# A decoder layer in f32r: SBUF tiles that begin at shifted addresses

## The chip, the core and the metric

The kernel runs on one core of a Trainium2 chip. A core has a matrix engine (TensorE, PE in the profile, with its weight loads shown as PEld), VectorE (DVE), ScalarE (ACT), GpSimd (POOL) and SyncE (SP), which here issues nearly all DMAs. Operands lie in SBUF, 128 partitions wide; an address below is a place in bytes within a partition, the same in all 128. TensorE writes to PSUM.

The metric is the time of the whole kernel on the device in microseconds, median of several runs.

## The reference

One layer over x of 256 positions and 1024 channels, with a LayerNorm behind each of three parts:

```python
x = layer_norm(ALPHA * x + 0.5 * swiglu(x, ffn1_w_up, ffn1_w_down), ln1_g, ln1_b)
z = x @ w_in                       # q, k, v, h, g_b, g_c, gates: 8192 columns
y_attn = moba_attention(q, k, v) @ w_proj_attn      # 8 heads of 128, causal, one block of 256
y_conv = (g_b * short_conv(g_c * h, conv_w, conv_b)) @ w_proj_conv   # 3 taps per channel
g_attn, g_conv = split(sigmoid(gates + b_gate))
x = layer_norm(ALPHA * x + (g_attn * y_attn + g_conv * y_conv) @ w_out, ln2_g, ln2_b)
x = layer_norm(ALPHA * x + 0.5 * swiglu(x, ffn2_w_up, ffn2_w_down), ln3_g, ln3_b)
# swiglu(x, w_up, w_down) = (silu(gate) * up) @ w_down, hidden width 2816
```

All inputs are float32, and the weights are read once: 119.56 MB from HBM.

## The kernel before

**Numbers in two parts.** Each float32 factor is split into a high part, rounded to the type float32r (f32r below), and a low part, the rest. A product is three f32r matmuls: high by high, high by low, low by high. ScalarE makes the high part by a cast, VectorE the low part by a subtraction. For weights that is `prep` (L884 and L887), from a raw tile that a DMA has filled into two S tiles, hi and lo. For activations it is `split` (L203, L204) and `split_later` (L213, L208), into X tiles or T tiles.

**Tiles.** A `Slots` object (L49) hands out tiles of one kind from a pool with a fixed number of places, in turn. S: 10 tiles of 2048 words (8192 bytes) for weights, and q and k of the attention. X: 3 tiles of 4096 words (16,384 bytes) for transposed activations and v. RAW: 3 tiles of 2048 words for weights as they come from HBM. N: 9 tiles of 1032 words (4128 bytes) for rows of x, LayerNorm vectors, gates and the convolution. T: 8 tiles of 512 words (2048 bytes) for small things, among them the hidden activations of a feed-forward part. In SBUF the ten S tiles stand one behind the other, then the X, raw and T tiles, then identity, mask and small constants, then the N tiles.

**Matmuls.** `cols` (L346) holds weight columns still and streams activations: per unit of weights 16 matmuls of 512 columns (hi weights against both parts of X) and 16 of 256 columns (lo weights against the high part); in the profile these are `acc<-X,S`, the moving operand first. `rows` (L294) holds activations still and streams 512 weight columns (`acc<-S,X`). The down projection `D` (L437) holds a T tile still and streams S (`acc<-S,T`). All these matmuls stand in line 117. Transposes (L190) are float32 matmuls against the identity (`acc<-ident,N` and `acc<-ident,T`). All f32r operands are slices that begin at a multiple of 512 bytes within their tile.

**The convolution.** In `GC` (L566) an N tile holds u, four channel tiles of 258 words each (1032 bytes, a multiple of 32 and 8 more), two zeros ahead of 256 positions. L574 writes u behind the two zeros, so 8 bytes into it. L578 (ScalarE) reads it from there for the last tap, and L582 (VectorE) reads it from its start and from one word on for the other two.

**Order.** The program is put in an order by hand: the matmuls stand in a list with a modelled time each, `advance` and `prep` (L879 to L919) issue casts and subtractions some time ahead of the matmuls that need them, `defer` puts steps a little later. A raw tile is loaded as soon as one of the three places is free (L869). Nothing in this depends on addresses.

Of the kernel before, what the change touches and what calls it, by code (L numbers as in the profile page):

```python
# [29 lines left out]
S_BUFS, X_BUFS, RAW_BUFS, N_BUFS, T_BUFS, ACC_BUFS = 10, 3, 3, 9, 8, 8  # L30


class Op:


    def __init__(self, fn, cols, unit=None):
        self.fn, self.cols, self.unit, self.after = fn, cols, unit, []
# [11 lines left out]
class Slots:  # L49


    def __init__(self, pool, tag, shape, bufs):
        self.pool, self.tag, self.shape, self.bufs, self.live, self.n = pool, tag, shape, bufs, 0, 0

    def get(self, dt=F):
        assert self.live < self.bufs, self.tag
        self.live += 1
        self.n += 1
        return self.pool.tile(self.shape, dt, tag=self.tag, name=f"{self.tag}{self.n}", bufs=self.bufs)

    def free(self, n=1):
        self.live -= n
# [3 lines left out]
def layer(ctx: ExitStack, tc: tile.TileContext, a: dict, out: bass.AP):  # L66
    nc = tc.nc
    sb = ctx.enter_context(tc.tile_pool(name="sb", bufs=1))
    ps = ctx.enter_context(tc.tile_pool(name="ps", bufs=1, space=PSUM))
    ctx.enter_context(tc.manual_schedule())  # L70

    S = Slots(sb, "S", [128, 2048], S_BUFS)
    X = Slots(sb, "X", [128, 4096], X_BUFS)
    RAW = Slots(sb, "raw", [128, 2048], RAW_BUFS)
    N = Slots(sb, "N", [128, 1032], N_BUFS)
    T = Slots(sb, "T", [128, 512], T_BUFS)
    ACC = Slots(ps, "acc", [128, 512], ACC_BUFS)

    base, ins, units, sig, st = [], [], [], [], {}
# [3 lines left out]

    for pool in (S, X, RAW, T):
        pool.get()
        pool.free()


    still = T.get(R)
    nc.gpsimd.memset(still.bitcast(F), 0.0)  # L90
# [21 lines left out]
    def small(shape, name, bufs=2):  # L112
        return sb.tile(shape, F, name=name, bufs=bufs)


    def mm(dst, lhsT, rhs, start, stop, cols, unit=None):
        return Op(lambda: nc.tensor.matmul(dst(), lhsT=lhsT(), rhs=rhs(), start=start, stop=stop), cols, unit)  # L117

    def passes(dst, sta, mov, first, last, cols, unit=None):

        return [mm(dst, lambda x=x: sta(x), lambda w=w: mov(w), first and i == 0, last and i == 2, cols, unit)
                for i, (x, w) in enumerate(((0, 0), (0, 1), (1, 0)))]
# [95 lines left out]
    def xnew():  # L218
        return X.get(R).rearrange("p (k s t n) -> p k s t n", k=KT, s=2, t=2)

# [154 lines left out]
    def both(dst, bank):  # L375
        nc.scalar.copy(dst, bank[:, 256:512])  # L376
        nc.vector.tensor_tensor(dst, dst, bank[:, 0:256], op=OP.add)  # L377


    def ffn(key, wu, wd, ln_i, by_rows, order, tail, after_ln):  # L380
# [4 lines left out]
        def hT_of(j, kk):  # L385
            if ("hT", key, j, kk) not in st:
                st["hT", key, j, kk] = T.get(R).rearrange("p (s n) -> p s n", s=2)
            return st["hT", key, j, kk]

        def U_epi(j, t, bank):  # L390
            sc = T.get()
            nc.scalar.activation(sc[:, 0:256], bank[:, 0:256], AF.Silu)
            nc.vector.tensor_tensor(sc[:, 256:512], sc[:, 0:256], bank[:, 256:512], op=OP.mult)
            st["h", j, t] = sc

        def hT_put(j, t, at, dt):
            def evac(bank):
                T.free()
                for kk in range(2):
                    hT = hT_of(j, kk)[:, :, t * 128:(t + 1) * 128]  # L400
                    split(hT[:, 0], hT[:, 1], bank[:, kk * 128:(kk + 1) * 128])
# [14 lines left out]
        def U_cols(j):  # L416
            ug, uu = col_unit(wu, j * 256), col_unit(wu, DFF + j * 256)

            def gate(bank, b):
                g = T.get()  # L420
                both(g[:, 0:256], bank)
                defer(0.8, lambda: nc.scalar.activation(g[:, 0:256], g[:, 0:256], AF.Silu))  # L422
                st["g", j, b] = g
# [10 lines left out]
            if j == NJ - 1:  # L434
                base[-1].after.append(X.free)

# [91 lines left out]
    def V(c, t):  # L528
# [3 lines left out]
        def epi(bank):  # L532
            if c == 0 and t == 0:
                st["v"] = X.get(R).rearrange("p (s t n) -> p s t n", s=2, t=2)
            cs = slice(c * 512, (c + 1) * 512)
# [11 lines left out]
    def QK(kind, c):  # L547
        def epi(bank, j):
            if j == 0:
                state["hold"] -= 1  # L550
                st[kind, c] = S.get(R).rearrange("p (s h n) -> p s h n", s=2, h=4)
            t_ = T.get()
# [65 lines left out]
    def attention(head, at, dt):  # L618
# [5 lines left out]
        def bank(name, lo, hi):  # L624
            def f():
                if name not in box:
                    box[name] = ACC.get()
                return box[name][:, lo:hi]
            return f


        both_k = lambda: st["k", c][:, :, h, 0:128]
        ops = [mm(bank("S", 0, 256), lambda: qT(0, 0, 128), both_k, True, False, 256),
               mm(bank("S", 0, 128), lambda: qT(1, 0, 128), lambda: kT(0, 0, 128), False, True, 128)]
        ops += passes(bank("S", 256, 512), lambda s: qT(s, 128, 256), lambda w: kT(w, 0, 256), True, True, 256)

        def softmax():
            if head == 0:
                st["xT", "a"] = xnew()
            P = T.get()  # L640
            b = box["S"]
            mx = small([128, 2], "mx")
# [5 lines left out]
            ACC.free()  # L648
            nc.vector.reduce_max(mx[:, 0:1], P[:, 0:128], axis=mybir.AxisListType.X)
            nc.vector.reduce_max(mx[:, 1:2], P[:, 128:384], axis=mybir.AxisListType.X)  # L650
            nc.vector.tensor_scalar(mx, mx, -1.0, None, op0=OP.mult)
# [205 lines left out]
    order, need, clock, t = [], {}, [], 0.0  # L857
# [99 lines left out]
```

## Time and profile before

| | |
|---|---|
| median of 2 runs | 644.17 us (644.11 and 644.24) |
| the profiled execution, its own time | 644.08 us |
| its span, first to last instruction | 642.3 us |
| TensorE busy (matmuls) | 632.6 us, 98% of the span |
| VectorE, ScalarE, GpSimd busy | 71%, 56%, 3% |
| mean granted TensorE clock | 0.996 of 2.4 GHz |

The page of a profile shows one execution: busy time by engine, the span in 40 slices, the chain of work that ended last, and groups of instructions by line. Matmuls are pipelined: one begins before the last has ended, so the shown length of one (283 or 389 ns) is longer than the distance from start to start, the pitch. A row of the timeline merges neighbours of a kind: its start, its length up to the end of the last of them, and how many they are (xN). PE is busy nearly always here, so what counts is the pitch. Rows of a stretch (A:B in us from the span's start) give each engine's busy time in it and, in brackets, the instructions that touch it.

### The profile page before, as it was taken

What the parts mean: (1) busy time and instruction counts of PE and PEld (TensorE: products, weight loads), DVE (VectorE), ACT (ScalarE), POOL (GpSimd) and SP (SyncE); (2) the same over time, 40 slices, a digit from 0 to 9 for tenths busy, and PEclk for the clock granted to TensorE, in tenths of its full rate; (3) what the DMA queues carried; (4) which work ended last, traced back from release to release, by engine and by line L of the source; (5) the groups of instructions that cost most, each with busy time, mean ns of one, the idle gap of its engine ahead of it and who ended that gap; (6) DMA issues with size and microseconds to landing.
All of it is one profiled execution on the core that took longest, in us unless ns stands there. A gap on an engine that the chain in (4) does not pass through costs nothing.

```text
span 642.3 us, 8774 instructions
## 1 busy us (share of the span) xinstructions
PE 632.6 (98%) x3416; PEld 547.3 (85%) x3416; DVE 454.3 (71%) x731; ACT 356.8 (56%) x624; POOL 18.7 (3%) x27
## 2 busy tenths in 40 slices
PE   8999999999999999999999999999999999999995
PEld 6888888888888888888888888888888888888884
DVE  4786666666678577778879987886966666666636
ACT  5765555555534558676698664552556555555510
POOL 2000000000011000000000000001100000000002
PEclk9999999999999999999999999999999999999998
DMA  9766665567635572555666655572556755555301
GB/s 294 259 233 199 218 234 193 204 218 254 193 124 180 157 234 85 158 171 163 204 214 193 222 201 181 197 257 77 190 196 207 253 196 197 197 196 197 132 1 66
DMA packets 95854, 121.18 MB, mean 189 GB/s; under 512 B 2196, under 2 KB 84420, under 8 KB 95812
## 3 DMA queue, kind: packets, MB, share of 16 engines
q1 hardware_dynamic: 95668, 120.36, 57.4%
q8 instruction: 27, 0.44, 0.3%
q10 hardware_dynamic: 144, 0.26, 0.1%
q14 instruction: 15, 0.12, 0.1%
HBM read 119.56 MB, written 1.05 MB: 188 GB/s over the span
## 4 chain that ended last, share of the span: by engine, by line
PE 98%; POOL 0%; DVE 0%; issue 0%; ACT 0%; POOLq 0%; DVEq 0%
PE acc L117 96%; PE acc L190 1%; PE acc L147 0%; POOL rs L250 0%; POOL nmr L821 0%; DVE S L887 0%; ACT X L203 0%; POOL T L90 0%; POOLq L953 0%; POOL N L824 0%; DVE bn L240 0%; DVE N L238 0%; DVE mv L246 0%; PE acc L717 0%; DVE ve L248 0%
## 5 line engine op out<-in xcount | busy, mean ns | idle before, releaser
L117 PE MATMUL acc<-X,S 128*128 128x256 f32 (+1 forms) x2368 | 419.9, 337 | 0.0
L117 PEld LDWEIGHTS acc<-X,S 128*128 128x128 f32 x2368 | 363.2, 190 | 47.0
L887 DVE TENSOR_TENSOR S<-raw,S 128x1024 fp32r<-128x1024 f32 (+1 forms) x224 | 268.0, 1205 | 47.9 <-ACT S L884 46.6
L884 ACT CAST S<-raw 128x1024 fp32r<-128x1024 f32 (+1 forms) x224 | 227.6, 1034 | 48.1 <-PE acc L117 42.9
L117 PE MATMUL acc<-S,T 128*128 128x512 f32 (+1 forms) x546 | 123.4, 382 | 0.0
L117 PEld LDWEIGHTS acc<-S,T 128*128 128x128 f32 x546 | 100.0, 188 | 19.8
L377 DVE TENSOR_TENSOR T<-T,acc 128x256 f32<-128x256 f32 x132 | 55.4, 419 | 79.7 <-ACT T L376 79.1
L376 ACT COPY T<-acc 128x256 f32<-128x256 f32 x132 | 49.0, 371 | 98.3 <-PE acc L117 98.3
L117 PE MATMUL acc<-S,X 128*128 128x512 f32 x336 | 80.0, 394 | 0.6 <-ACT S L884 0.3
L117 PEld LDWEIGHTS acc<-S,X 128*128 128x128 f32 x336 | 62.2, 188 | 13.8 <-DVE S L887 0.8
L213 ACT CAST T<-T 128x256 fp32r<-128x256 f32 x38 | 15.5, 407 | 24.9 <-DVE T L428 24.6
L422 ACT ACTIVATE T<-T 128x256 f32<-128x256 f32 x38 | 15.9, 418 | 14.3 <-DVE T L377 14.3
L203 ACT CAST X<-acc 128x512 fp32r<-128x512 f32 x16 | 9.4, 587 | 22.6 <-PE acc L190 14.3
L204 DVE TENSOR_TENSOR X<-acc,X 128x512 fp32r<-128x512 f32 x16 | 10.9, 686 | 12.4 <-ACT X L203 12.3
L238 DVE SCALAR_TENSOR_TENSOR N<-acc,N 128x512 f32<-128x512 f32 (+1 forms) x13 | 8.4, 643 | 15.5 <-PE acc L117 15.5
L250 POOL TENSOR_TENSOR rs<-ve,mhalf 128x1 f32<-128x1 f32 x6 | 5.8, 964 | 460.4 <-DVE ve L248 460.4
L208 DVE TENSOR_TENSOR T<-T,T 128x256 fp32r<-128x256 f32 x38 | 15.9, 419 | 1.9 <-ACT T L213 1.9
L428 DVE TENSOR_TENSOR T<-T 128x256 f32<-128x256 f32 x38 | 16.2, 425 | 1.3
L203 ACT CAST T<-acc 128x128 fp32r<-128x128 f32 (+1 forms) x28 | 8.2, 293 | 15.1 <-DVE T L204 14.1
L377 DVE TENSOR_TENSOR N<-N,acc 128x256 f32<-128x256 f32 x24 | 10.0, 417 | 5.6 <-ACT N L376 5.6
L213 ACT CAST X<-T 128x256 fp32r<-128x256 f32 x16 | 6.5, 407 | 12.1 <-DVE T L377 6.8
L204 DVE TENSOR_TENSOR T<-acc,T 128x128 fp32r<-128x128 f32 (+1 forms) x28 | 9.1, 326 | 5.4 <-ACT T L203 5.4
(72 smaller groups left out, 213.0 us busy)
## 6 DMA issues: line engine op xcount, KB each, us to landing
raw<-in_ffn_w_up SPq DMA_DIRECT2D x38, 1024.0 KB, 5.1
raw<-in_w_in SPq DMA_DIRECT2D x32, 1024.0 KB, 5.5
raw<-in_ffn_w_down SPq DMA_DIRECT2D x22, 1024.0 KB, 4.9
raw<-in_w_proj_attn SPq DMA_DIRECT2D x4, 1024.0 KB, 5.3
raw<-in_w_proj_conv SPq DMA_DIRECT2D x4, 1024.0 KB, 5.0
raw<-in_w_out SPq DMA_DIRECT2D x4, 1024.0 KB, 4.9
raw<-in_ffn_w_up SPq DMA_DIRECT2D x8, 512.0 KB, 4.7
raw<-in_ffn_w_up SPq DMA_DIRECT2D x8, 256.0 KB, 5.6
```

Of the source, the lines that this page charges most:

```text
L117: return Op(lambda: nc.tensor.matmul(dst(), lhsT=lhsT(), rhs=rhs(), start=start, stop=stop), cols, unit)
L203: nc.scalar.copy(hi, src)
L204: nc.vector.tensor_tensor(lo, src, hi.bitcast(F), op=OP.subtract)
L208: nc.vector.tensor_tensor(lo, src, hi.bitcast(F), op=OP.subtract)
L213: nc.scalar.copy(hi, src)
L238: nc.vector.scalar_tensor_tensor(y[:, c], src, scale, st["ax", t][:, c], op0=OP.mult, op1=OP.add)
L376: nc.scalar.copy(dst, bank[:, 256:512])
L377: nc.vector.tensor_tensor(dst, dst, bank[:, 0:256], op=OP.add)
L422: defer(0.8, lambda: nc.scalar.activation(g[:, 0:256], g[:, 0:256], AF.Silu))
L428: nc.vector.tensor_tensor(g[:, 0:256], g[:, 0:256], g[:, 256:512], op=OP.mult)
L884: nc.scalar.copy(u.hi[:, s], u.raw[:, s])
L887: nc.vector.tensor_tensor(u.lo[:, s], u.raw[:, s], u.hi[:, s].bitcast(F), op=OP.subtract)
```

## The change

`Slots` gets a number `spread`. Where it is not 0, each place in the pool is 8 words (32 bytes) longer, and the tile handed out is a slice of it that begins `n * spread % 8` words behind the place's start, n counting the tiles handed out of this kind. S gets 3, X gets 1, T gets 5; RAW and N stay. The starts in turn are, for S, 24, 4, 16, 28, 8, 20, 0, 12 bytes and over again; for X, 8, 12, 16 and so on up to 28, 0, 4; for T, 8, 28, 16, 4, 24, 12, 0, 20.

The places of S then lie 8224 bytes apart, those of X 16,416, those of T 2080. Raw tiles begin 320 + 96 = 416 bytes later than before, identity, constants and N tiles 672 bytes later. The instructions of each engine, their order and the waits of each are those of before.

```diff
-    def __init__(self, pool, tag, shape, bufs):
+    def __init__(self, pool, tag, shape, bufs, spread=0):
         self.pool, self.tag, self.shape, self.bufs, self.live, self.n = pool, tag, shape, bufs, 0, 0
+        self.spread = spread
 
     def get(self, dt=F):
         assert self.live < self.bufs, self.tag
         self.live += 1
         self.n += 1
-        return self.pool.tile(self.shape, dt, tag=self.tag, name=f"{self.tag}{self.n}", bufs=self.bufs)
+        p, n = self.shape
+        t = self.pool.tile([p, n + 8 * (self.spread > 0)], dt, tag=self.tag, name=f"{self.tag}{self.n}", bufs=self.bufs)
+        if not self.spread:
+            return t
+        o = self.n * self.spread % 8
+        return t[:, o:o + n]
...
-    S = Slots(sb, "S", [128, 2048], S_BUFS)
-    X = Slots(sb, "X", [128, 4096], X_BUFS)
+    S = Slots(sb, "S", [128, 2048], S_BUFS, 3)
+    X = Slots(sb, "X", [128, 4096], X_BUFS, 1)
     RAW = Slots(sb, "raw", [128, 2048], RAW_BUFS)
     N = Slots(sb, "N", [128, 1032], N_BUFS)
-    T = Slots(sb, "T", [128, 512], T_BUFS)
+    T = Slots(sb, "T", [128, 512], T_BUFS, 5)
```

## Rows read from the trace of the kernel before

**Rows 1.** Head of the page: busy us, share, instructions; chain that ended last.
```profile
span 642.3 us, 8774 instructions
PE 632.6 (98%) x3416; PEld 547.3 (85%) x3416; DVE 454.3 (71%) x731; ACT 356.8 (56%) x624; POOL 18.7 (3%) x27
...
PE acc L117 96%; PE acc L190 1%; PE acc L147 0%; POOL rs L250 0%; POOL nmr L821 0%; DVE S L887 0%; ACT X L203 0%; POOL T L90 0%; POOLq L953 0%; POOL N L824 0%; DVE bn L240 0%; DVE N L238 0%; DVE mv L246 0%; PE acc L717 0%; DVE ve L248 0%
```
**Rows 2.** Waits of PE: us in total, times, longest.
```profile
PE acc L147 <- POOL T L90: 1.3, 1, 1.3
PE acc L117 <- ACT S L884: 0.3, 1, 0.3
PE acc L117 <- DVE S L887: 0.3, 1, 0.3
```
**Rows 3.** Groups by line and shape: busy us, mean ns | idle before.
```profile
L117 PE MATMUL acc<-X,S 128*128 128x512 f32 x1184 | 288.9, 392 | 0.0
L887 DVE TENSOR_TENSOR S<-raw,S 128x1024 fp32r<-128x1024 f32 x216 | 262.6, 1224 | 46.3 <-ACT S L884 45.1
L884 ACT CAST S<-raw 128x1024 fp32r<-128x1024 f32 x216 | 222.8, 1049 | 46.2 <-PE acc L117 42.9 <-DMA raw<-in_ffn_w_up 2.8 <-DMA raw<-in_w_in 0.5
L117 PE MATMUL acc<-X,S 128*128 128x256 f32 x1184 | 154.6, 283 | 0.0
L117 PE MATMUL acc<-S,T 128*128 128x512 f32 x510 | 119.1, 389 | 0.0
L117 PE MATMUL acc<-S,X 128*128 128x512 f32 x336 | 80.0, 394 | 0.6 <-ACT S L884 0.3 <-DVE S L887 0.3
```
**Rows 4.** Timeline of PE, two runs of one shape: start us, us, engine.
```profile
286.21 1.36 PE L117 MATMUL acc<-X,S 128*128 128x256 f32 x10
...
295.67 2.66 PE L117 MATMUL acc<-X,S 128*128 128x512 f32 x11
```
**Rows 5.** Two stretches by engine, and PE's timeline in each.
```profile
core 0: us, PE busy (x) PEld busy (x) DVE busy (x) ACT busy (x) POOL busy (x), PEclk, DMA share, GB/s
620.40:625.00 4.60, 4.60 (x22) 3.82 (x21) 0.00 (x0) 0.00 (x0) 0.00 (x0) 1.00 0.00 0
109.66:112.32 2.66, 2.66 (x13) 2.23 (x12) 2.66 (x4) 2.50 (x4) 0.00 (x0) 1.00 0.97 327
...
620.06 5.15 PE L117 MATMUL acc<-S,T 128*128 128x512 f32 x22
...
109.66 2.66 PE L117 MATMUL acc<-S,T 128*128 128x512 f32 x11
```
**Rows 6.** Transposes of L190: duration ns min/median/max, first and last start.
```profile
L190 PEld LDWEIGHTS acc<-ident,N x48: 137/140/230, 3.6 to 460.1; 128*128 128x128 f32 x48
L190 PE MATMUL acc<-ident,N x48: 270/272/422, 4.0 to 460.2; 128*128 128x128 f32 x48
L190 PEld LDWEIGHTS acc<-ident,T x36: 138/139/144, 21.7 to 479.4; 128*128 128x128 f32 x36
L190 PE MATMUL acc<-ident,T x36: 270/272/276, 21.8 to 479.5; 128*128 128x128 f32 x36
```
**Rows 7.** Instructions on N tiles, same columns.
```profile
L582 DVE SCALAR_TENSOR_TENSOR N<-N,cvec,N x16: 476/482/485, 336.8 to 365.0; 128x256 f32<-128x256 f32 x16
...
L574 DVE TENSOR_TENSOR N<-T,N x8: 424/426/428, 333.2 to 362.1; 128x256 f32<-128x256 f32 x8
L578 ACT ACTIVATE N<-N,cvec x8: 589/602/602, 334.3 to 362.6; 128x256 f32<-128x256 f32 x8
...
L762 DVE TENSOR_TENSOR N<-N,T x8: 424/424/427, 387.2 to 417.6; 128x256 f32<-128x256 f32 x8
```
**Rows 8.** DMA queue of SP (share of 16 engines), weight loads, ScalarE's waits for them.
```profile
q1 hardware_dynamic: 95668, 120.36, 57.4%
...
raw<-in_w_in SPq DMA_DIRECT2D x32, 1024.0 KB, 5.5
raw<-in_ffn_w_down SPq DMA_DIRECT2D x22, 1024.0 KB, 4.9
...
raw<-in_ffn_w_up SPq DMA_DIRECT2D x8, 256.0 KB, 5.6
...
ACT S L884 <- DMA raw<-in_ffn_w_up: 4.7, 4, 2.1
ACT S L884 <- DMA raw<-in_w_in: 0.5, 1, 0.5
```

## The prediction

> **What bounds the kernel now.** I read four views in this order. The head of the page first [rows 1]: TensorE is busy for 98% of the span of 642.3 us at the full granted clock (a mean of 0.996; 1.00 is the level of 2.4 GHz), and the chain that ended last is 98% TensorE, 96% of it the matmuls of L117. Then TensorE's waits [rows 2]: 1.3 + 0.3 + 0.3 = 1.9 us in the whole run, so nothing that another engine or a DMA does later or sooner is felt, unless it is much later. Then the matmuls by shape [rows 3]: 1184 + 510 + 336 of 512 columns and 1184 of 256 carry the run. Last, their pitch, from the timeline [rows 4]. Ten of 256 columns take 1.36 us, and the last of them is 0.283 us long [rows 3], so the pitch is (1.36 - 0.283) / 9 = 120 ns. Eleven of 512 columns take 2.66 us, so (2.66 - 0.389) / 10 = 227 ns. At 2.4 GHz the columns alone need 107 and 213 ns. The kernel is therefore columns, plus about 13 ns in each matmul whether it is long or short.
>
> So the change can be worth something in one way only: it must alter the pitch of a matmul. The address of an operand is all that it alters. There are two sides to that. An address could make two readers or a reader and a writer of SBUF meet less often (a gain), or make one operand take longer to read (a loss).
>
> **The change part by part.** The order of the instructions on each engine, and what each waits for, is the same before and after; nothing is added, removed or moved. The three parts are addresses.
>
> *Tiles 32 bytes farther apart.* Before, all S, X and T tiles begin at the same place modulo 128 bytes, since their sizes are multiples of 2048 bytes and they lie one behind the other. If they collided there, a matmul beside busy VectorE, ScalarE and DMA would be slower than one beside nothing. The trace has both [rows 5]. From 620.4 to 625.0 us VectorE, ScalarE, GpSimd and the DMA engines did nothing at all, and 22 matmuls of this shape took 5.15 us: (5.15 - 0.389) / 21 = 226.7 ns. From 109.66 to 112.32 us VectorE was busy all the time, ScalarE for 2.50 of 2.66 us, both with S tiles, and the DMA engines for 97%: (2.66 - 0.389) / 10 = 227.1 ns. The difference is 0.4 ns, which is the rounding of the rows. I take 0 for what collisions with other engines cost. At the other end, the group means differ between 389 ns (S,T) and 392 ns (X,S), and if those 3 ns were collisions, 1184 x 3 ns = 3.6 us could come back; that end I keep for the range.
>
> What is left is a collision between TensorE's own two readers, the weight load and the moving operand; all f32r operands of this kernel are at multiples of 512 bytes from each other, so no row shows the other case for them. The nearest rows are the f32 transposes [rows 6]. Their weights come from N tiles, which are 4128 bytes and so lie 32, 64 or 96 bytes behind a multiple of 128 relative to the identity, or from T tiles, which lie at 0. The weight load takes a median of 140 ns from the one and 139 ns from the other, the matmul 272 ns from both. So I take 0 here as well.
>
> *A start of 0 to 28 bytes behind the place.* VectorE and ScalarE have done this before in the short convolution, where the tile u is read and written behind its start [rows 7]. The 16 L582 read u at 0 or 4 bytes plus 8 bytes per channel tile, so at every offset of 4 from 0 to 28: all of them take 476 to 485 ns. The eight L574 write at 8, 16, 24 and 0 bytes and take 424 to 428 ns; L762, all aligned, takes 424 to 427. The eight L578 on ScalarE read at the same four offsets, 0 among them: 589 to 602 ns. So these two engines pay nothing, and if they paid some ns, the 1.9 us of waits of TensorE say that it is hidden by the lead of the weight preparation. TensorE has never read an f32r operand from such an address here. Its bounds: nothing, as on the two other engines; or one further fetch, taken as four words (half of the eight-word range in which the change shifts its tiles), so four columns of 1 / 2.4 GHz = 0.417 ns, 1.7 ns in a matmul; far out, half pace, 0.417 ns more per column. I take nothing, since three kinds of reads and writes in this trace, on two engines, show no dependence.
>
> [...]
>
> *The other tiles move along.* S, X and T grow by 320, 96 and 256 bytes in all, so raw tiles begin 416 bytes later and the rest 672 bytes later, still at multiples of 32 bytes, but raw no longer at multiples of 64. The DMA engines' weight packets take 57% of their time [rows 8], and ScalarE waited for a landing for 5.2 us in all. [...] I take 0 and keep 0.2 us for the upper end.
>
> The sum: 0 + 0 + 0. The profiled execution took 644.08 us, 1.78 us more than its span; the median of the two runs shown is 644.17, so I forecast 644.2.
>
> **The rivals.** *No change*, 0.80: everything within the runs' own scatter, 643.5 to 645.
>
> *A further line for each moving read* (slower, by less than 2%), 0.07. Of the eight starts of a tile, two are multiples of four words; a count over the changed program gives 2455 of its 3331 f32r moving reads off such a multiple. 2455 x 1.7 ns = 4.2 us, with the 0.2 us of the first loads 648.6 us. It would be 2% from 12.9 us / 2455 = 5.3 ns each. For it: TensorE takes a word every 0.417 ns, faster than the engines that were seen not to care. Against it: L582, L574 and L578. [...]
>
> *TensorE loses half its reading pace on odd words* (slower by more than 2%), 0.07. The place is the moving read of an S or X tile that begins 4, 12, 20 or 28 bytes behind its place: 555,264 of the program's 1,385,520 columns. If the array is fed two words at a time and only from an even word, these columns take 0.417 ns more each: 555,264 x 0.417 ns = 231 us, so 875 us. A loss of 0.023 ns per such column, an eighteenth of that, already makes the 12.9 us of 2%. For it: that the array takes 2.4 words in a ns, where VectorE and ScalarE take 1024 words in 1224 and 1049 ns [rows 3], so their rows say little about a reader at this pace. Against it: the transposes, whose weights begin at several places, though none off a multiple of eight words [rows 6].
>
> *The two readers of TensorE part* (faster), 0.06. If the 13 ns that every matmul has beyond its columns were its weight load and its moving operand meeting at the same place of SBUF, up to 3331 x 13 ns = 43 us would go, to 601 us; with half of it 623 us. From 12.9 us / 3331 = 3.9 ns per matmul it is 2%. For it: the 13 ns are the same for long and short matmuls, as one weight load each would make them. Against it: the transposes, whose two operands lie at several distances, show no difference [rows 6].
>
> **How the numbers follow.** The likeliest is 644.2 us. Two in ten are to be left out at most: the far slow rival and the gain of tens of us (together 0.13) lie outside, the further line inside. The range goes from 644.2 - 3.6 = 640.6 (the 3 ns of the X,S group) to 648.6 for the further line, rounded up to 649. What a measurement of this kernel can tell from no change is taken as 2%. Faster by over 2%: 0.06, of which I put 0.01 to gains that stay below, so 0.05. Slower by over 2%: the half pace, 0.07. The rest, 0.88, is within 2%.
>
> **What would show it.** In the changed kernel's profile, the pitch decides each step: 120 and 227 ns again for runs of 256 and 512 columns means that addresses do nothing; 122 and 229 the further line; up to 227 and 440, in some runs and not in others, the lost pace; 113 and 220 or less the parted readers. L887 should stay at 1224 ns and L884 at 1049 ns, TensorE's waits at about 2 us, and the median landing of a weight load at 4.9 to 5.5 us. I am wrong if matmuls of one shape fall into classes by the start of their tile.

## The result, and the profile after

The changed kernel takes **653.21 us** (653.16 to 653.27), the kernel before 644.17 us: a ratio of 1.014, 95% interval [1.0124, 1.0156]. That is 9.0 us slower, outside the forecast range of 640.6 to 649.0 us. The verdict by 2% is "same", but the loss is several times the width of the interval.

The head of the page and TensorE's waits answer to [rows 1, 2].

```profile
span 651.4 us, 8774 instructions
PE 641.5 (98%) x3416; PEld 548.6 (84%) x3416; DVE 454.7 (70%) x731; ACT 357.1 (55%) x624; POOL 18.7 (3%) x27
...
PE acc L156 <- POOL T L99: 1.3, 1, 1.3
PE acc L126 <- ACT S L893: 0.5, 1, 0.5
PE acc L126 <- DVE S L896: 0.3, 1, 0.3
```

The span grew by 9.1 us, TensorE's busy time by 8.9 us (641.5 against 632.6), its waits by 0.2 us. Nothing waits more; the matmuls themselves take longer. The groups by shape, which answer to [rows 3] (every line number is 9 higher now, so L126 is the old L117):

```profile
L126 PE MATMUL acc<-X,S 128*128 128x512 f32 x1184 | 293.4, 395 | 0.0
L896 DVE TENSOR_TENSOR S<-raw,S 128x1024 fp32r<-128x1024 f32 x216 | 262.8, 1225 | 47.9 <-ACT S L893 46.7
L893 ACT CAST S<-raw 128x1024 fp32r<-128x1024 f32 x216 | 222.5, 1047 | 48.8 <-PE acc L126 45.5 <-DMA raw<-in_ffn_w_up 2.9 <-DMA raw<-in_w_in 0.4
L126 PE MATMUL acc<-X,S 128*128 128x256 f32 x1184 | 153.9, 281 | 0.0
L126 PE MATMUL acc<-S,T 128*128 128x512 f32 x510 | 122.4, 396 | 0.0
L126 PE MATMUL acc<-S,X 128*128 128x512 f32 x336 | 82.2, 400 | 0.8 <-ACT S L893 0.5 <-DVE S L896 0.3
```

One matmul of 512 columns is 3, 7 and 6 ns longer than before (395, 396, 400 against 392, 389, 394), one of 256 columns 2 ns shorter. VectorE and ScalarE need what they needed (1225 and 1047 ns). From all start-to-start times of the trace, the sums by kind are: X past S of 512 columns 276.3 us against 271.7, of 256 columns 141.1 against 141.8, S past T 119.2 against 115.8, S past X 80.4 against 78.2. That is +4.5 - 0.7 + 3.4 + 2.2 = 9.4 us, all of the loss (the remaining kinds took 0.3 us less).

The stretch beside which nothing else runs, as in [rows 5], by engine and on TensorE's timeline:

```profile
628.90:634.20 5.30, 5.30 (x24) 4.30 (x23) 0.00 (x0) 0.00 (x0) 0.00 (x0) 1.00 0.00 0
...
628.63 5.79 PE L126 MATMUL acc<-S,T 128*128 128x512 f32 x24
```

VectorE, ScalarE, GpSimd and the DMA engines are still (the zeros), the clock is granted in full (1.00), and the pitch is (5.79 - 0.396) / 23 = 234.5 ns, where it was 226.7. So TensorE alone is slower, at the same clock, beside nobody.

### The profile page after: what moved, and what is told of

Its sections match the earlier page's. It is cut to its first block, busy times and chain, and to the rows that moved or that the text cites. A ratio compares the mean times of both kernels' runs of the same rounds, so it can differ in the third digit from the quotient of the medians.

```text
span 651.4 us, 8774 instructions
## 1 busy us (share of the span) xinstructions
PE 641.5 (98%) x3416; PEld 548.6 (84%) x3416; DVE 454.7 (70%) x731; ACT 357.1 (55%) x624; POOL 18.7 (3%) x27
## 4 chain that ended last, share of the span: by engine, by line
PE 98%; POOL 0%; DVE 0%; issue 0%; ACT 0%; POOLq 0%; DVEq 0%
PE acc L126 96%; PE acc L199 1%; PE acc L156 0%; POOL rs L259 0%; POOL nmr L830 0%; DVE S L896 0%; ACT X L212 0%; POOL T L99 0%; POOLq L962 0%; POOL N L833 0%; DVE bn L249 0%; DVE N L247 0%; DVE mv L255 0%; PE acc L726 0%; DVE ve L257 0%
## 5 line engine op out<-in xcount | busy, mean ns | idle before, releaser
L126 PE MATMUL acc<-X,S 128*128 128x256 f32 (+1 forms) x2368 | 423.8, 338 | 0.0
L126 PEld LDWEIGHTS acc<-X,S 128*128 128x128 f32 x2368 | 364.1, 189 | 49.9
L896 DVE TENSOR_TENSOR S<-raw,S 128x1024 fp32r<-128x1024 f32 (+1 forms) x224 | 268.1, 1206 | 49.6 <-ACT S L893 48.4
L126 PE MATMUL acc<-S,T 128*128 128x512 f32 (+1 forms) x546 | 126.7, 388 | 0.0
L126 PEld LDWEIGHTS acc<-S,T 128*128 128x128 f32 x546 | 100.5, 189 | 22.6
L126 PE MATMUL acc<-S,X 128*128 128x512 f32 x336 | 82.2, 400 | 0.8 <-ACT S L893 0.5
L126 PEld LDWEIGHTS acc<-S,X 128*128 128x128 f32 x336 | 62.4, 189 | 15.8 <-ACT S L893 0.9
L212 ACT CAST X<-acc 128x512 fp32r<-128x512 f32 x16 | 9.4, 589 | 23.4 <-PE acc L199 14.4
```

Source lines behind the costliest of these rows:

```text
L212: nc.scalar.copy(hi, src)
L896: nc.vector.tensor_tensor(u.lo[:, s], u.raw[:, s], u.hi[:, s].bitcast(F), op=OP.subtract)
```

## The experiments

Each ratio is to the kernel before, run beside it on the same chip (644.16 to 644.30 us there). The pitches in the table are means over all matmuls of a kind, in ns from start to start; S past X contains the start of the kernel and its waits. "Distance" is how far the moving operand lies from the still one.

| run | us | ratio, 95% interval | X past S, 512 | X past S, 256 | S past T, 512 | S past X, 512 |
|---|---|---|---|---|---|---|
| before | 644.17 | | 229.5 | 119.8 | 227.1 | 232.8 |
| the change | 653.21 | 1.0140 [1.0124, 1.0156] | 233.3 | 119.2 | 233.7 | 239.3 |
| e1 spacing alone | 650.65 | 1.0098 [1.0083, 1.0113] | 233.1 | 118.3 | 232.2 | 238.1 |
| e2 S alone | 651.89 | 1.0116 [1.0101, 1.0132] | 232.8 | 118.8 | 233.6 | 238.0 |
| e3 X alone | 652.58 | 1.0129 [1.0114, 1.0144] | 233.1 | 119.0 | 234.3 | 239.2 |
| e4 T alone | 647.50 | 1.0047 [1.0030, 1.0064] | 229.8 | 119.8 | 232.1 | 234.5 |
| e5 all 96 bytes on | 644.08 | 0.9999 [0.9990, 1.0009] | 229.5 | 119.7 | 227.1 | 232.9 |
| e6 T 96 bytes on | 648.19 | 1.0062 [1.0047, 1.0077] | 229.9 | 119.8 | 234.3 | 233.8 |
| e7 low parts 64 off | 645.37 | 1.0018 [1.0009, 1.0027] | 231.1 | 117.0 | 229.9, low 231.2 | 235.1, low 236.1 |
| e8 X starts, places even | 647.98 | 1.0058 [1.0043, 1.0073] | 232.0 | 119.1 | 227.6 | 236.4 |
| e9 T 32 | 647.75 | 1.0053 [1.0038, 1.0068] | 229.7 | 119.8 | 233.4 | 233.0 |
| e10 T 128 | 647.55 | 1.0050 [1.0035, 1.0065] | 229.8 | 119.8 | 233.1 | 233.4 |
| e11 T 256 | 644.11 | 1.0000 [0.9990, 1.0009] | 229.5 | 119.7 | 227.1 | 232.9 |
| e12 T 512 | 644.31 | 1.0000 [0.9991, 1.0010] | 229.5 | 119.8 | 227.1 | 234.2 |
| e13 eight S tiles, even | 653.12 | 1.0141 [1.0125, 1.0156] | 229.5 | 119.7 | 227.1 | 262.3 |
| e14 e13, all 4 bytes on | 676.51 | 1.0496 [1.0478, 1.0513] | 240.2 | 122.3 | 238.0 | 269.9 |
| e17 e13, all 8 bytes on | 663.67 | 1.0295 [1.0273, 1.0317] | 233.9 | 120.1 | 232.8 | 265.3 |
| e15 e13, all 12 bytes on | 656.48 | 1.0190 [1.0175, 1.0205] | 230.9 | 119.9 | 229.3 | 259.8 |
| e18 e13, all 16 bytes on | 656.60 | 1.0188 [1.0170, 1.0206] | 231.6 | 117.6 | 230.3 | 268.8 |
| e16 e13, starts in turn | 659.21 | 1.0238 [1.0219, 1.0257] | 232.5 | 118.9 | 232.5 | 259.8 |

**Which part, and start or distance (e1 to e4).** e1 keeps the 32 bytes of spacing and drops the starts; e2 to e4 do both for one kind of tile:

```diff
-        o = self.n * self.spread % 8
+        o = 0                              # e1
...
-    S = Slots(sb, "S", [128, 2048], S_BUFS, 3)
+    S = Slots(sb, "S", [128, 2048], S_BUFS)    # e3: X alone; T likewise
```

> 

> The places of S, X and T stand 32 bytes farther apart, but every tile begins at its place (starts are multiples of 32 bytes). [...] Theory B (what matters is where a weight load stands relative to the moving operand that streams beside it; before, the two were always a multiple of 512 bytes apart): they now differ by multiples of 32 bytes, so slower, 648 to 653 us, with pitches of 512 columns from 227 to 240 ns. Theory C (each tile's start off a multiple of 64 bytes costs, for either operand): about half of the loss, 648 to 649 us.

> 

> Only S tiles are spaced and shifted, X and T as before. From the pitches of before and of the change, the 510 matmuls that stream S past a T tile lost 6.6 ns each, the 336 that stream S past X lost 6.5 ns, the 1184 of 512 columns that stream X past S lost 3.8 ns. [...] Theory B: every matmul has S as one of its operands, so all lose, about 653 us, and X past S of 512 columns goes to some 233 ns.

> 

> Only X tiles are spaced and shifted. [...] Theory B: X past S and S past X both lose, 4.5 - 0.7 + 2.2 = 6.0 us, so 650.2 us; S past T keeps 227.1 ns.

> 

> Only T tiles are spaced and shifted; in the large matmuls T is only ever the still operand. [...] Theory B: the 510 matmuls S past T lose some 6.6 ns each, 3.4 us, so 647.6 us, with their pitch at 230 to 234 ns; the others keep theirs.

e1 costs 6.4 us with every tile at a multiple of 32 bytes, and e4 slows S past T by 5 ns with T only ever the still operand. So the start of the moving operand can't be all of it; theory B holds for both. Two groups of e1, then one of e4:

```profile
L126 PE MATMUL acc<-X,S 128*128 128x512 f32 x1184 | 293.2, 395 | 0.0
L126 PE MATMUL acc<-S,T 128*128 128x512 f32 x510 | 121.7, 394 | 0.0
...
L126 PE MATMUL acc<-S,T 128*128 128x512 f32 x510 | 121.6, 394 | 0.0
```

The parts don't add up (e2, e3 and e4 lose 7.6, 8.3 and 3.2 us), and e3 shows one reason. Its groups:

```profile
L126 PE MATMUL acc<-X,S 128*128 128x512 f32 x1184 | 293.1, 395 | 0.0
L126 PE MATMUL acc<-X,S 128*128 128x256 f32 x1184 | 153.7, 281 | 0.0
L126 PE MATMUL acc<-S,T 128*128 128x512 f32 x510 | 122.7, 396 | 0.0
```

S past T went from 389 to 396 ns, though neither S nor T was changed, which I had not expected. But the three X tiles grew by 96 bytes, so T, behind them, came to lie 96 bytes off against S.

**Distance or address (e5, e6).** One unused tile of 96 bytes, ahead of S or ahead of T:

```diff
     for pool in (S, X, RAW, T):
+        if pool is S:                      # e6: T
+            sb.tile([128, 24], F, name="fill")
         pool.get()
```

> 

> An unused tile of 96 bytes ahead of the S tiles: every S, X, raw and T tile begins 96 bytes later, and all distances among them are those of before. Theory B (the distance between the still and the moving operand): no change, 644.2 us, pitch 227 ns for S past T. Theory C (where an operand begins in SBUF by itself, here 224 in place of 128 bytes behind a multiple of 512): slower, 648 us or more.

> 

> The unused tile of 96 bytes stands between the raw and the T tiles: T begins at the same addresses as with the tile ahead of everything, S and X stay where they were. In the run with X alone, where T also came to lie 96 bytes off against S, S past T took 234.3 ns per matmul in place of 227.1. Theory B: the same again, 510 x 7.2 ns = 3.7 us, so 647.9 us, and no other kind of matmul slower. Theory C: T lies where it lies in the run with everything moved, so the same time as that run.

T has the same addresses in both. In e5 everything moves together and nothing is lost. In e6, where T alone is off, S past T takes 234.3 ns, to the tenth the value of e3, and the time is 648.19 us where 647.9 was expected. The groups of e5, then of e6:

```profile
L119 PE MATMUL acc<-X,S 128*128 128x512 f32 x1184 | 288.9, 392 | 0.0
L119 PE MATMUL acc<-S,T 128*128 128x512 f32 x510 | 119.1, 390 | 0.0
```

```profile
L119 PE MATMUL acc<-X,S 128*128 128x512 f32 x1184 | 289.4, 392 | 0.0
L119 PE MATMUL acc<-S,T 128*128 128x512 f32 x510 | 122.7, 397 | 0.0
```

Only the group whose two operands moved against each other is clearly longer: 7.2 ns in the pitch, the other kinds at most 1.0. Its stretch with the other engines still, by engine and on the timeline of e6:

```profile
624.30:629.40 5.10, 5.10 (x23) 4.09 (x23) 0.00 (x0) 0.00 (x0) 0.00 (x0) 1.00 0.00 0
...
624.11 5.55 PE L119 MATMUL acc<-S,T 128*128 128x512 f32 x23
```

(5.55 - 0.397) / 22 = 234.2 ns beside nothing, so it lies between TensorE's own two operands. Theory C falls for this shift: a start 96 bytes farther on costs nothing by itself.

**A gain at some distance? (e7, e8).** In e1 to e4 some matmuls of 256 columns had got faster, so e7 puts the low parts alone 64 bytes off:

```diff
-    S = Slots(sb, "S", [128, 2048], S_BUFS)
+    L = Slots(sb, "L", [128, 2048], S_BUFS // 2)
+    S = Slots(sb, "S", [128, 2048], S_BUFS // 2)
...
-            u.hi, u.lo = S.get(R), S.get(R)
+            u.hi, u.lo = S.get(R), L.get(R)
```

> 

> The S tiles are handed out from two rings of five, one for low parts (and k), one for high parts (and q), and an unused tile of 64 bytes stands between the rings, so that the low parts alone lie 64 bytes off against X and T. Theory B, with the pitches by distance in the runs so far: matmuls of 256 columns, which hold low parts still, 119.8 to some 116.5 ns at a distance of 64 bytes, 1184 x 3.3 = 3.9 us less; the third of S past T and S past X that streams low parts some 4.4 ns more, 282 x 4.4 = 1.2 us; together 641.5 us, faster than the kernel before. Theory D (the distance of a multiple of 512 bytes is best for every matmul): the ones of 256 columns lose too, 646 us or more.

> 

> X alone begins 0 to 28 bytes behind its places, as in the change, but its places stand 256 bytes farther apart and an unused tile of 256 bytes follows, so that S and T keep their distances and X is off by the small starts alone, or by 256 bytes more. Theory B at full strength: 512 columns of X past S and S past X lose as with X alone in the earlier run, 3.6 and 6 ns, 4.3 + 2.0 us, less 0.9 us at 256 columns, so 649.5 us, with S past T back at 227 ns. Theory B by blocks of 32 bytes or more (small starts don't matter): 644 to 646 us.

e7 failed as a faster version: 1.2 us slower where 2.7 us were to be won. The gain came (256 columns: 119.8 to 117.0 ns, 3.2 us), but X past S of 512 columns, whose operands kept their distance, lost 1.6 ns each, 1.9 us, and S past T and S past X lost 2.5 us, more than their low third should. The groups of e7:

```profile
L120 PE MATMUL acc<-X,S 128*128 128x512 f32 x1184 | 290.8, 394 | 0.0
L120 PE MATMUL acc<-X,L 128*128 128x256 f32 x1184 | 151.5, 279 | 0.0
L120 PE MATMUL acc<-S,T 128*128 128x512 f32 x340 | 108.6, 392 | 0.0
L120 PE MATMUL acc<-L,T 128*128 128x512 f32 x170 | 67.0, 394 | 0.0
```

S past T is longer (392 against 389) with both its operands at their old distance; what differs is the matmul ahead of or behind it, L past T. So a pair off its distance is also paid for by other matmuls, and not by the next one alone: in X past S the loss lies in the first ten matmuls behind a block of 256 columns (the first takes 237.8 ns where it took 233.4, the eighth 228.6 where it took 226.9) and is gone from the eleventh on (at most 226.8). Why is not settled.

e8 gives X the starts alone (places longer by 64 words in place of 8, and an unused tile of 64 words ahead of the raw tiles). It loses 3.8 us, less than theory B at full strength but far from nothing, and S past T is back at 227.6 ns. So a few bytes count too, but e8 can't tell whether as a distance or as a start. Sorted by the start of X, the moving operand, X past S of 512 columns takes 229.3 ns at 0 bytes, 233.6 at 8, 231.3 at 12, 239.2 at 20 and 232.7 at 24; the still S tiles all begin at multiples of 32 bytes here.

**How far (e9 to e12).** e6 with 32, 128, 256 or 512 bytes in place of 96.

> 

> T lies 32 bytes off against S and X, in place of 96. Theory B1 (any distance other than a multiple of 512 bytes costs): in the runs so far S past T at this distance stood at about 232 ns where it was 227.1, so 510 x 5 = 2.6 us, 646.8 us. Theory B2 (a distance costs by its part below 128 bytes): the same here.

> 

> T lies 128 bytes off. Theory B1: as at 32 bytes, 646 to 647 us, S past T at about 232 ns. Theory B2: 644.2 us, 227 ns.

> 

> T lies 256 bytes off. Theory B1: 646 to 647 us, S past T at about 231 ns. Theory B2: 644.2 us, 227 ns.

> 

> T lies 512 bytes off, so all f32r operands are again multiples of 512 bytes apart. Theories B1 and B2: 644.2 us, 227 ns. If it is slower, what matters is not the distance modulo 512 bytes but the very distance of before, or the growth of SBUF in use.

32 and 128 bytes cost 3.5 and 3.3 us, 256 and 512 nothing. Neither B1 (256 costs) nor B2 (128 is free) was right: of the distances tried for S past T, the multiples of **256 bytes** are free and the others are not. S past T in e10 and in e11:

```profile
L119 PE MATMUL acc<-S,T 128*128 128x512 f32 x510 | 122.1, 395 | 0.0
```

```profile
L119 PE MATMUL acc<-S,T 128*128 128x512 f32 x510 | 119.1, 389 | 0.0
```

**The start by itself (e13 to e18).** Eight S tiles make room for places 256 bytes farther apart, so that one common start leaves all distances at multiples of 256 bytes:

```diff
-S_BUFS, X_BUFS, RAW_BUFS, N_BUFS, T_BUFS, ACC_BUFS = 10, 3, 3, 9, 8, 8
+S_BUFS, X_BUFS, RAW_BUFS, N_BUFS, T_BUFS, ACC_BUFS = 8, 3, 3, 9, 8, 8
...
-        t = self.pool.tile([p, n + 8 * (self.spread > 0)], ...
+        t = self.pool.tile([p, n + 64 * (self.spread > 0)], ...
...
-        o = self.n * self.spread % 8
+        o = 0          # e13; e14: 1, e17: 2, e15: 3, e18: 4; e16: as in the change
```

> 

> Eight S tiles in place of ten, and the places of S, X and T 256 bytes farther apart: all distances are multiples of 256 bytes. A base for the next three runs: the pitches 227 and 120 ns as before; the time 644 us, or somewhat more if TensorE waits for weights with fewer S tiles.

> 

> As e13, and every S, X and T tile begins 4 bytes behind its place, so the distances are kept. Theory B (distance alone): the time and pitches of e13. [...]

> 

> As e13, and every S, X and T tile begins 12 bytes behind its place. Theory B: the time of e13. [...]

> 

> As e13, with the change's starts of 0 to 28 bytes in turn and no 32-byte spacing. Theory B: distances of -28 to 28 bytes, nearly all off, so slower than e13 by about what spacing alone cost, 5 to 9 us. If a few bytes within 32 don't count as a distance: the time of e13.

> 

> As e13, every tile begins 8 bytes behind its place. If the cost falls with the words that are left in the first 16 bytes (4 bytes: 11 ns per matmul of 512 columns, 12 bytes: 2 ns), it lies between, some 6 ns, 2030 x 6 = 12 us more than e13, 665 us. If it is a matter of odd words alone: the time of e13, 653 us.

> 

> As e13, every tile begins 16 bytes behind its place. With 16 bytes as the unit: the time and pitches of e13, 653 us. With 32 bytes as the unit: slower by several us, pitches of 512 columns above 227 ns.

e13 itself is 8.8 us slower than the kernel before for a reason of its own, fewer weight tiles: TensorE now waits 6.3 us for L896, while the pitches of the first three kinds are those of before. Behind the first of two such waits close together, of 2.25 and 1.70 us, its granted clock also fell below 1.00 for part of ten microseconds (means of 0.64 and 0.67 in the two stretches below; an estimate from them: (0.36 + 0.33) x 5 = 3.5 us lost). The wait, two stretches and two groups of e13:

```profile
PE acc L126 <- DVE S L896: 6.3, 4, 2.2
...
460.00:465.00 5.00, 3.23 (x9) 2.21 (x10) 3.06 (x5) 3.21 (x4) 0.92 (x1) 0.64 0.61 210
465.00:470.00 5.00, 5.00 (x20) 4.00 (x19) 2.06 (x3) 0.59 (x1) 0.00 (x0) 0.67 0.87 289
...
L126 PE MATMUL acc<-X,S 128*128 128x512 f32 x1184 | 288.9, 392 | 0.0
L126 PE MATMUL acc<-S,T 128*128 128x512 f32 x510 | 119.1, 389 | 0.0
```

So these runs are read against e13 (e17 and e18 ran on another chip than e13 to e16). The profiles of e14, e15, e17 and e18 have such falls too, not equally long, and that of e16 has none there (mean granted clock 0.992, 0.994, 0.992 and 0.990, and 0.997 in e16); they lie in stretches of S past X. A difference of 2 or 3 us between the times of these runs can therefore be the clock's, and the pitches of the first three kinds are the surer measure. A common start of 4 bytes costs 23.4 us, of 8 bytes 10.6, of 12 bytes 3.4, of 16 bytes 3.5; S past T goes from 227.1 to 238.0, 232.8, 229.3 and 230.3 ns. The 4 ns that separate the starts in the changed kernel (236.2 against 232.2 ns at 4 bytes behind a multiple of 16 and at one) would give 2030 x 4 ns = 8 us at 4 bytes, a third of what came. The groups of e14:

```profile
L126 PE MATMUL acc<-X,S 128*128 128x512 f32 x1184 | 301.5, 402 | 0.0
L126 PE MATMUL acc<-X,S 128*128 128x256 f32 x1184 | 157.7, 287 | 0.0
L126 PE MATMUL acc<-S,T 128*128 128x512 f32 x510 | 124.6, 400 | 0.0
```

So the start counts by itself, and theory B alone falls as well. Here both operands begin at the same start, but the prices are nearly those of e8, where only the moving operand's start was off: X past S takes 240.2, 233.9 and 230.9 ns at 4, 8 and 12 bytes, against 239.2, 233.6 and 231.3 there at 20, 8 and 12. In the changed kernel, too, S past T follows the start of the moving S (232.1, 236.8, 234.5 and 232.0 ns at 0, 4, 8 and 12 bytes behind a multiple of 16) and not that of the still T (233.7 and 233.6 at 4 and 8, where nearly all of them begin). So this price goes with the moving operand's start. What a start of a few bytes costs in the still operand can't be told from the distance that it makes. One further fetch of four words, the prediction's estimate, doesn't fit either: by it starts of 4, 8 and 12 bytes would cost the same and one of 16 bytes nothing, and they cost 11, 6, 2 and 3 ns in S past T. In e5 a shift by 96 bytes, three times 32, was free. e16, the change's starts without its spacing, costs 6.1 us against e13, within the 5 to 9 expected. Its X past S takes 239.0 ns at a start of X of 20 bytes, as in e8, and 232.0 at 0, where only the still S tiles begin off their places (229.3 in e8).

## Why the prediction was wrong, point by point

- *Only the pitch of a matmul can matter.* Right: waits of 2.1 us, and the pitches hold all of the 9 us.
- *Collisions with VectorE, ScalarE and DMA cost nothing.* Right: the loss is there in full in the stretch where all of them are still, in the changed kernel and in e6. The 3 ns between X past S and S past T that were kept for the range were no collisions either: in the kernel before, X past S takes 226.6 to 227.0 ns from the sixth matmul behind a block of 256 columns on, and 228.4 to 235.7 in the first five.
- *Tiles 32 bytes farther apart: "So I take 0 here as well."* This is the step that failed. It is 6.4 us (e1). The prediction saw the place, TensorE's weight load and its moving operand, but took its price from the float32 transposes, and no matmul of the kind in question had ever run at another distance. The transposes show nothing after the change either (a median weight load of 141 and 142 ns, a matmul of 272 ns from both N and T), while the f32r matmuls lose up to 7 ns. They were no measure for them. An unknown that no row shows should have had a bound on the slow side too; it got one on the fast side only.
- *Starts behind the place.* Right for VectorE and ScalarE: in the changed kernel L591 (the old L582) takes 477 to 486 ns, L587 (L578) 592 to 604. Wrong for TensorE, where "I take nothing" stood on those two engines. In the change the starts add 2.6 us to the spacing (653.21 against 650.65 in e1); with one start for all they cost 3.4 to 23.4 us.
- *Raw tiles at 32 bytes.* Right: e5 moves them by 96 bytes and takes 644.08 us; ScalarE waits 5.3 us for DMAs after the change, 5.2 before [rows 8]. The 0.2 us of the upper end were the author's estimate; no run shows them.
- *The rivals.* "A further line" had the sign and, at 648.6 us, half of the loss, but neither the mechanism nor its signs: it asked for 122 and 229 ns, and the trace has 119 and 233. No run shows its 1.7 ns, four words, for every read off a multiple of four words: S past T pays 11, 6 and 2 ns at common starts of 4, 8 and 12 bytes (e14, e17, e15). "The two readers part" had the right place and the wrong sign: of the distances tried for S past T, the even ones of before were the best, not the worst. "Half the pace on odd words" did not come: 4 bytes for all cost 11 ns in a matmul of 512 columns, not 213.
- The last line of the prediction held: it named classes by the start of a tile as what would show it wrong, and in the changed kernel the matmuls of 512 columns whose moving read begins 4 bytes behind a multiple of 16 have a mean pitch 4 ns above those that begin at one (236.2 against 232.2 ns). It named no price for the distance, which is the larger part.

What stays open: what in the chip makes the distance count. Weight loads do run beside the matmuls (PEld is busy for 4.30 of 5.30 us in the changed kernel's stretch with the other engines still), but that the two get into each other's way was not shown, only the distance was. Open too are the share that the neighbours of a matmul pay (e7), and why matmuls of 256 columns gain 2 to 3 ns at some distances, and at a start of 16 bytes with all distances even (117.6 ns in e18). For S past T only distances with T moved farther on were tried. In e1, X past S of 512 columns with the same distance in the three matmuls ahead and the next one takes 229.6 ns at 0 and 229.3 where X lies 64 bytes on from S, against 232.8 to 234.2 at the six other distances; no run puts all tiles there.

## What to carry to other kernels

Keep the operands of f32r matmuls at multiples of 32 bytes (common starts of 4 to 16 bytes cost 3.4 to 23.4 us in e14, e15, e17 and e18, one of 96 bytes nothing in e5), the moving one above all (X past S 239.2 ns at 20 bytes against 229.3 at 0 in e8), and the still and the moving operand at a multiple of 256 bytes from each other (32, 96 and 128 bytes cost 3.3 to 4.0 us in e9, e6 and e10, 256 and 512 nothing in e11 and e12; both measured on 512 columns); tiles of a size that is a multiple of 256 bytes, one behind the other, do this by themselves, and one odd tile between two kinds (96 bytes in e6) undoes it for kinds that nobody touched. Before changing an address, write down which distances change with it, those of the tiles behind it included. And where a price is unknown, a row of another kind of instruction is no zero: bound it on both sides.

## What the runs showed of the hardware

- At a granted clock of 1.00, 256 columns more in an f32r matmul take 107 ns (pitches of 227 and 120 ns in the kernel before, [rows 4]): 2.4 columns in a ns.
- With all other engines still, the pitch of an f32r matmul of 512 columns (S past T) is 226.7 ns where its two operands lie 256 or 512 bytes off their old distance (e11, e12), and 233.3, 234.2 and 232.4 ns at 32, 96 and 128 bytes (e9, e6, e10).
- At equal distances it is 227, 238, 233, 229 and 230 ns for starts of 0, 4, 8, 12 and 16 bytes behind a multiple of 32 bytes (e13, e14, e17, e15, e18), and the price goes with the moving operand's start (e8).
- Matmuls of 256 columns pay less for a start (from 120 to 122 ns at 4 bytes) and gain at some distances (117 ns at 64 bytes in e7).
- VectorE and ScalarE show no price for a start of 0 to 28 bytes: 477 to 486 and 592 to 604 ns over all starts in the convolution, and 1225 and 1047 ns for the preparation of weights in the changed kernel, where it was 1224 and 1049.
